# A transformer trunk in split float32r on one Trainium2 core: the weight tiles moved through all sixteen pairs of offsets modulo 128 bytes

## The chip, the cores and the metric

The kernel runs on one core of one Trainium2 chip. The metric is device time in microseconds (us) of one execution, from its first instruction to its last with what the device adds around them; smaller is better. Two timed executions of the kernel before took 2649.68 and 2650.5 us, median 2650.09 us.

## The reference

A decoder trunk of two layers, 256 tokens of width 2048, all float32. Layer 0 mixes tokens by retention (8 heads), layer 1 by sliding-window attention with sinks (32 query heads of 64, 4 key/value heads); each layer then has a SwiGLU feed-forward part (hidden width 5632) and a gated per-layer embedding (PLE, width 256):

```python
for i in range(DEPTH):
    h = rmsnorm(x, norm_mix[i])
    if i % N_MIXERS == 0:
        x = x + retention_mixer(h, ret_w_in[j], ret_gn[j], ret_w_out[j])
    else:
        x = x + swa_mixer(h, swa_w_in[j], swa_sinks[j], swa_w_out[j])
    x = x + swiglu(rmsnorm(x, norm_ffn[i]), ffn_w_in[i], ffn_w_out[i])
    gate = jax.nn.sigmoid(rmsnorm(x, norm_ple[i]) @ ple_w_gate[i])
    x = x + gate * (p[i] @ ple_w_proj[i])
return rmsnorm(x, norm_final)
```

Nearly all of the arithmetic is in the seven kinds of weight product: `ret_w_in` (2048 x 12288), `ret_w_out` (4096 x 2048), `swa_w_in` (2048 x 2560), `swa_w_out` (2048 x 2048), and per layer `ffn_w_in` (2048 x 11264), `ffn_w_out` (5632 x 2048), `ple_w_gate` (2048 x 2048) and `ple_w_proj` (256 x 2048).

## The kernel before

**Split operands.** A float32 matrix is split exactly into two float32r parts, hi and lo. A product of two matrices is then three TensorE products: hi by hi, hi by lo, lo by hi (L159 to L161 of `multiply`).

**Units.** A weight is cut into chunks of 512 output columns, and a chunk into units of 256 rows, 128 x 1024 float32 values in SBUF (512 KB). A unit takes one DMA on SP's queue into a `raw` tile (`load`, L125), one ScalarE activation that writes `hi` (L208) and one VectorE subtraction that writes `lo` (L209, both from `split_weights`, L133), and twelve matmuls: two blocks of 128 rows, two token tiles of 128, three products. In each of the twelve, 128 columns of the transposed activation are the stationary operand (loaded with an LDWEIGHTS of its own), and 512 columns of `hi` or `lo` are the moving one, one row of 2048 bytes in each partition. The stationary pairs are `xTh`/`xTl` (the normalised residual, for every product from the trunk), `yTh`/`yTl` (into `ret_w_out`), `hTh`/`hTl` (into `ffn_w_out`), `oTh`/`oTl` (into `swa_w_out`) and `pTh`/`pTl` (into `ple_w_proj`); each is an `Lhs` object, the trunk's with a new object per norm on the same two tiles.

**Order.** `run` (L163) goes through all units in one fixed order, one stage after another; loads are issued five units ahead (`LOADS`), splits three ahead (`AHEAD`), and after each unit one step of the side work is taken: transposes of finished chunks on VectorE (L233), norms, attention. Engines meet by semaphores on tiles that the tile pools hand out: five `raw`, four `hi`, four `lo`.

**Where tiles lie.** Every partition of SBUF is one address range; the pools take their tiles from it in the order in which they are opened, each tile rounded up to 32 bytes. `xs`, `ident`, `gains` and `gn` are multiples of 128 bytes long. `mhalf` (L103) has 16 bytes and takes 32, so that everything behind it, `xTh`, `xTl`, `pTh`, `pTl`, `raw`, `hi` and `lo`, starts 32 bytes past a multiple of 128. The pool `small` shifts what follows by 32 more: `xt`, `yT`, `hT`, `oT` and the retention's tiles start 64 bytes past a multiple of 128. Token tiles, row blocks and units are multiples of 512 bytes, so that an operand keeps its tile's offset in each matmul. In what follows, the offset of a tile is its address modulo 128 bytes, and the difference is the stationary operand's offset minus the moving one's, modulo 128.

The places that matter here are the pools and tiles at the head of `tile_trunk` (L90 to L106), `split_weights` (L133 to L139), `run`'s first lines (L166), the tiles of `yT`, `oT` and `hT` in the `opened` functions of `retention`, `swa` and `ffn`, and the tile `qkT` of a head's transposed queries and keys in `retention` (L318).

Of the kernel before, what the change touches and what calls it, by code (L numbers as in the profile page):

```python
# [11 lines left out]
F32 = mybir.dt.float32  # L12
# [6 lines left out]
P = 128  # L19
# [24 lines left out]
class Lhs:  # L44
    """A transposed activation, split exactly into two float32r parts."""

    def __init__(self, tiles=None):
        self.tiles = tiles
        self.ready = set()
# [5 lines left out]
class Chunk:  # L55
    """512 output columns for all tokens, accumulated over the whole contraction, in pieces of
    a token tile and some of the columns."""
# [7 lines left out]
class Unit:  # L65
    """KU blocks of 128 rows of a weight, in one chunk's columns."""

    def __init__(self, chunk, src, kts, lhs):
        self.chunk, self.src, self.kts, self.lhs = chunk, src, kts, lhs
        self.w = None  # L70


class Stage:
    """A part of the trunk with tiles of its own, from its first unit to its last."""
# [4 lines left out]
    def linear(self, w, block, lhs, done, units=None, chunk=None):  # L79
        """One chunk: block of 512 columns of a weight laid out by `_units`."""  # L80
        ch = chunk or Chunk(self, done)
        for u in units if units is not None else range(w.shape[1]):
            self.units.append(Unit(ch, w[block, u], range(KU * u, KU * u + KU), lhs))
            ch.left += 1
# [3 lines left out]
def tile_trunk(ctx, tc, ins, out):  # L88
    nc = tc.nc
    pool = ctx.enter_context(tc.tile_pool(name="persist", bufs=1))  # L90
    wraw = ctx.enter_context(tc.tile_pool(name="wraw", bufs=5))
    whi = ctx.enter_context(tc.tile_pool(name="whi", bufs=4))
    wlo = ctx.enter_context(tc.tile_pool(name="wlo", bufs=4))
    small = ctx.enter_context(tc.tile_pool(name="small", bufs=4))
# [3 lines left out]

    xs = pool.tile([P, NT, D], F32, name="xs")
# [3 lines left out]
    mhalf = pool.tile([P, 4], F32, name="mhalf")  # L103
    turned = ctx.enter_context(tc.tile_pool(name="turned", bufs=1))
    xT = [pool.tile([P, KD, S], F32R, name=n) for n in ("xTh", "xTl")]
    pT = [pool.tile([P, PLE_K, S], F32R, name=n) for n in ("pTh", "pTl")]  # L106

    # ---------------------------------------------------------------- streams
# [24 lines left out]
    def split_weights(u):  # L133
        raw = u.w
        hi = whi.tile([P, KU, NW], F32R, name="hi")
        lo = wlo.tile([P, KU, NW], F32R, name="lo")
        for part in u.parts:
            split(hi[:, part, :], lo[:, part, :], raw[:, part, :])
        u.w = (hi, lo)  # L139

    def multiply(u, which, left):
        """The unit's products for some pieces of its chunk; `left` of the chunk's units are
        still to come."""
        ch = u.chunk
        need(u.lhs, u.kts)
        if ch.acc is None:
            ch.acc = []
            for n, (_, cols) in enumerate(ch.pieces):
                bank, name = (ps_acc, "acc") if n < NT else (ps_at, "at")
                ch.acc.append(bank.tile([P, NW], F32, name=name)[:, : cols.stop - cols.start])  # L150
        hi, lo = u.w
        for j, k in enumerate(u.kts):
            first = not ch.begun and j == 0
            last = left == 0 and j == KU - 1
            for n in which:
                t, cols = ch.pieces[n]
                sl = slice(t * P, (t + 1) * P)
                xh, xl = u.lhs.hi[:, k, sl], u.lhs.lo[:, k, sl]
                nc.tensor.matmul(ch.acc[n], xh, hi[:, j, cols], start=first, stop=False)  # L159
                nc.tensor.matmul(ch.acc[n], xh, lo[:, j, cols], start=False, stop=False)  # L160
                nc.tensor.matmul(ch.acc[n], xl, hi[:, j, cols], start=False, stop=last)  # L161

    def run(stages, begin):  # L163
        """All units in order, their weights AHEAD units ahead; between them, steps of side work.
        The products of the units that end the last chunk go piece by piece of its output."""
        units = [(st, u) for st in stages for u in st.units]  # L166
        for n, (_, u) in enumerate(units[:LOADS]):
            if n < AHEAD:
                next(begin)
            load(u, 1 if n else KU)  # L170
            if n < AHEAD:
                split_weights(u)
        side.append(begin)
        now = None
        pools = ExitStack()
        last = [u for _, u in units[-AHEAD - 1 :]]
        assert len({id(u.chunk) for u in last}) == 1
        for i, (st, u) in enumerate(units):
            if st is not now:
                pools.close()  # L180
                st.open_(st, pools)
                now = st
            if i + LOADS < len(units):
                load(units[i + LOADS][1])
            if i + AHEAD < len(units):
                split_weights(units[i + AHEAD][1])
            if u is last[0]:
                break
            ch = u.chunk
            ch.left -= 1  # L190
            multiply(u, range(len(ch.pieces)), ch.left)
            ch.begun = True
            if ch.left == 0:
                g = ch.done(ch.acc)
                if g is not None:
                    side.append(g)
            step_side()
        ch = last[0].chunk
        for n, (t, cols) in enumerate(ch.pieces):
            for i, u in enumerate(last):  # L200
                multiply(u, [n], len(last) - 1 - i)
            ch.done(ch.acc[n], t, cols)
        pools.close()

    # ------------------------------------------------------------ small pieces
# [10 lines left out]
    def transpose_pair(srcs):  # L216
        """Two [128, 128] blocks of both token tiles -> a PSUM tile [128, 2, S]."""
        tr = ps_tr.tile([P, 2, S], F32, name="tr")
        for j, pair in enumerate(srcs):
            for t in range(NT):  # L220
                nc.tensor.transpose(tr[:, j, t * P : (t + 1) * P], pair[t], ident)
        return tr

    def transposes(dst, src):
        """Steps that transpose src [128, NT, 512] into dst [128, 4, S], by blocks of 32 x 32."""
# [11 lines left out]
    def blocks(src, i):  # L237
        """Blocks 2i and 2i + 1 of 128 columns of both token tiles."""
        return [[src(t)[:, b * P : (b + 1) * P] for t in range(NT)] for b in (2 * i, 2 * i + 1)]

    class Norm:
        """Sums of squares of the residual's chunks, and the transposed residual times the gain.
        The scale by token, inv, is applied behind the product with the weights."""
# [23 lines left out]
        def places(self, c, src):  # L267
            """Steps that put a chunk's four transposed blocks in place."""
            for j in range(4):
                if j % 2 == 0:  # L270
                    yield
                self.place(4 * c + j, src[:, j, :])
# [5 lines left out]
    def residual(stage, norm, c):  # L278
        """A chunk of an output projection onto the residual, then the next norm's part."""
# [16 lines left out]
    # --------------------------------------------------------------- retention  # L296
    def retention(norm, next_norm, w_in, w_out):
        yl = Lhs()

        def opened(st, pools):  # L300
            st.pool = pools.enter_context(tc.tile_pool(name="ret", bufs=2, reuse_waits="tile"))
            yl.tiles = [st.pool.tile([P, RET_OUT_K, S], F32R, name=n, bufs=1) for n in ("yTh", "yTl")]
# [3 lines left out]
        def head(h):  # L306
            st = {}

            def qk_done(acc):
# [7 lines left out]
                def later():  # L317
                    qkT = rp.tile([P, 4, S], F32, name="qkT", bufs=1)  # L318
# [77 lines left out]
    # ---------------------------------------------------- sliding-window attention  # L396
    def swa(norm, next_norm, w_in, w_out):
        ol = Lhs()
        st = {}

        def opened(stage, pools):
            sp = stage.pool = pools.enter_context(tc.tile_pool(name="swa", bufs=1, reuse_waits="tile"))
            ol.tiles = [sp.tile([P, KD, S], F32R, name=n) for n in ("oTh", "oTl")]
# [30 lines left out]
        def q_done_of(j):  # L434
            def q_done(acc):
# [12 lines left out]
                def scores(i):  # L448
                    """Of heads 2i and 2i + 1: the numerators and denominators' parts."""
# [100 lines left out]
        # The first chunks' last units wait for the last group of heads.  # L550
# [9 lines left out]
    # --------------------------------------------------------------------- FFN  # L560
    def ffn(layer, norm, next_norm):
        hl = Lhs()

        def opened(stage, pools):
            fp = stage.pool = pools.enter_context(tc.tile_pool(name="ffn", bufs=1, reuse_waits="tile"))
            hl.tiles = [fp.tile([P, FF_K, S], F32R, name=n) for n in ("hTh", "hTl")]
# [53 lines left out]
    # --------------------------------------------------------------------- PLE  # L620
    def ple(layer, norm, next_norm, final):
# [12 lines left out]
        def pair(c):  # L634
# [3 lines left out]
            def gate_done(acc):  # L638
# [7 lines left out]
                def later():  # L646
                    # The last reads of the old operand are queued: its place is free.
# [36 lines left out]
            def gate_last(acc, t, cols):  # L684
                """A piece of the last chunk; with a token tile's last one, its rows go out."""
# [39 lines left out]
    # ------------------------------------------------------------------- trunk  # L725
# [15 lines left out]
    def load_x():  # L741
        """The first norm's operand comes transposed, in step with the first chunk's weights."""
# [20 lines left out]
def _constants():  # L763
    """Tables that follow from the shapes alone."""
# [15 lines left out]
def _units(w):  # L780
    """[K, N] -> [N / 512, K / 256, 128, 2, 512]: each unit in one piece, by partitions."""
# [4 lines left out]
def _heads(w):  # L786
    """The retention's columns by heads: q and k, v, g."""
# [47 lines left out]
```

## Time and profile before

| what | value |
|---|---|
| median of the timed executions | 2650.09 us (2649.68 to 2650.5) |
| profiled execution, span from first to last instruction | 2647.9 us, 31279 instructions |
| TensorE busy (PE) | 2629.2 us, 99% of the span, 11632 matmuls |
| weight loads of TensorE (PEld) | 2142.7 us, 81% |
| VectorE (DVE) | 1817.2 us, 69% |
| ScalarE (ACT) | 1223.7 us, 46% |
| granted TensorE clock, mean of the core | 0.999 |
| DMA: share of the 16 engines' time of SP's queue | 58.5% |

The profiled execution's span is 2.2 us less than the median of the timed executions; those 2.2 us lie around the instructions. A matmul's duration in the profile is that of one instruction in a pipeline (0.39 us here) and overlaps its neighbours'; how fast matmuls follow each other is read from their starts, or from how many of them lie in a stretch in which TensorE is busy throughout. An LDWEIGHTS shows in the row PEld, and runs beside the matmul before the one that needs it.

### The profile page before, as it was taken

What the parts mean: (1) busy time and instruction counts of PE and PEld (TensorE: products, weight loads), DVE (VectorE), ACT (ScalarE), POOL (GpSimd) and SP (SyncE); (2) the same over time, 40 slices, a digit from 0 to 9 for tenths busy, and PEclk for the clock granted to TensorE, in tenths of its full rate; (3) what the DMA queues carried; (4) which work ended last, traced back from release to release, by engine and by line L of the source; (5) the groups of instructions that cost most, each with busy time, mean ns of one, the idle gap of its engine ahead of it and who ended that gap; (6) DMA issues with size and microseconds to landing.
All of it is one profiled execution on the core that took longest, in us unless ns stands there. A gap on an engine that the chain in (4) does not pass through costs nothing.

```text
span 2647.9 us, 31279 instructions
## 1 busy us (share of the span) xinstructions
PE 2629.2 (99%) x11632; PEld 2142.7 (81%) x11632; DVE 1817.2 (69%) x2567; ACT 1223.7 (46%) x1527; POOL 14.6 (1%) x30
## 2 busy tenths in 40 slices
PE   8999999999999999999999999999999999999998
PEld 6888888888888888888888887777888888888887
DVE  6777777766666667676555786888757575755565
ACT  6444444444444444444444555555444444444444
POOL 0000000000000000000000000000000000000000
PEclk9999999999999999999999999999999999999999
DMA  8555555565566565656655655346666666555564
GB/s 277 185 185 186 185 186 183 181 190 184 194 192 193 191 197 190 198 186 197 190 187 187 190 193 169 121 135 202 189 198 189 197 194 194 192 188 187 189 207 144
DMA packets 140506, 497.79 MB, mean 188 GB/s; under 512 B 15809, under 2 KB 19009, under 8 KB 140225
## 3 DMA queue, kind: packets, MB, share of 16 engines
q1 hardware_dynamic: 140064, 495.73, 58.5%
q8 instruction: 91, 1.49, 0.2%
q14 instruction: 63, 0.51, 0.1%
q10 hardware_dynamic: 288, 0.07, 0.0%
HBM read 493.63 MB, written 2.10 MB: 187 GB/s over the span
## 4 chain that ended last, share of the span: by engine, by line
PE 95%; DVE 3%; issue 1%; DMA 1%; ACT 0%; SPq 0%; ACTq 0%; POOLq 0%; POOL 0%; DVEq 0%
PE acc L159 31%; PE acc L161 31%; PE acc L160 31%; DVE lo L209 1%; DVE xt L233 1%; PE at L454 1%; PE tr L506 0%; PE at L532 0%; DMA raw<-in_ret_w_in 0%; PE at L323 0%; DVE xTl L212 0%; DVE qkT L233 0%; DMA xs<-in_x 0%; PE at L350 0%; PE at L352 0%
## 5 line engine op out<-in xcount | busy, mean ns | idle before, releaser
L209 DVE TENSOR_TENSOR lo<-raw,hi 128x1024 fp32r<-128x1024 f32 (+1 forms) x929 | 1131.8, 1221 | 720.2 <-ACT hi L208 712.8
L208 ACT ACTIVATE hi<-raw 128x1024 fp32r<-128x1024 f32 (+1 forms) x929 | 982.0, 1058 | 1210.9 <-PE acc L161 1117.4
L159 PE MATMUL acc<-hi,xTh 128*128 128x512 f32 x2592 | 1011.0, 390 | 6.6 <-ACT hi L208 5.4
L161 PE MATMUL acc<-hi,xTl 128*128 128x512 f32 x2592 | 1008.0, 389 | 0.8 <-DVE xTl L212 0.6
L160 PE MATMUL acc<-lo,xTh 128*128 128x512 f32 x2592 | 1008.7, 389 | 0.0
L159 PEld LDWEIGHTS acc<-hi,xTh 128*128 128x128 f32 x2592 | 487.3, 188 | 111.6 <-ACT hi L208 5.6
L161 PEld LDWEIGHTS acc<-hi,xTl 128*128 128x128 f32 x2592 | 487.0, 188 | 103.6 <-DVE xTl L212 2.5
L160 PEld LDWEIGHTS acc<-lo,xTh 128*128 128x128 f32 x2592 | 487.3, 188 | 100.5 <-issue 0.7
L161 PE MATMUL acc<-hi,hTl 128*128 128x512 f32 x704 | 278.4, 396 | 0.0
L160 PE MATMUL acc<-lo,hTh 128*128 128x512 f32 x704 | 278.4, 395 | 0.0
L159 PE MATMUL acc<-hi,hTh 128*128 128x512 f32 x704 | 278.4, 395 | 0.0
L233 DVE STREAM_TRANSPOSE xt<-h 32x256 f32<-32x256 f32 x352 | 153.6, 436 | 6.8
L161 PEld LDWEIGHTS acc<-hi,hTl 128*128 128x128 f32 x704 | 132.2, 188 | 32.1
L160 PEld LDWEIGHTS acc<-lo,hTh 128*128 128x128 f32 x704 | 132.2, 188 | 32.1
L159 PEld LDWEIGHTS acc<-hi,hTh 128*128 128x128 f32 x704 | 132.2, 188 | 31.9
L233 DVE STREAM_TRANSPOSE xt<-xs 32x256 f32<-32x256 f32 x320 | 139.5, 436 | 6.0
L161 PE MATMUL acc<-hi,yTl 128*128 128x512 f32 x256 | 101.2, 396 | 0.0
L160 PE MATMUL acc<-lo,yTh 128*128 128x512 f32 x256 | 101.2, 395 | 0.0
L159 PE MATMUL acc<-hi,yTh 128*128 128x512 f32 x256 | 101.2, 395 | 0.0
L233 DVE STREAM_TRANSPOSE qkT<-qk 32x256 f32<-32x256 f32 x128 | 55.8, 436 | 10.2 <-ACT qk L315 8.1
L211 ACT ACTIVATE xTh<-xt,gains 128x256 fp32r<-128x256 f32 x80 | 35.8, 499 | 56.0 <-DVE xt L233 51.6
L159 PEld LDWEIGHTS acc<-hi,yTh 128*128 128x128 f32 x256 | 48.1, 188 | 11.7
(124 smaller groups left out, 1178.2 us busy)
## 6 DMA issues: line engine op xcount, KB each, us to landing
raw<-in_ffn_w_in SPq DMA_DIRECT2D x352, 512.0 KB, 4.2
raw<-in_ret_w_in SPq DMA_DIRECT2D x191, 512.0 KB, 3.6
raw<-in_ffn_w_out SPq DMA_DIRECT2D x176, 512.0 KB, 4.0
raw<-in_ret_w_out SPq DMA_DIRECT2D x64, 512.0 KB, 4.0
raw<-in_ple_w_gate SPq DMA_DIRECT2D x64, 512.0 KB, 3.8
raw<-in_swa_w_in SPq DMA_DIRECT2D x40, 512.0 KB, 3.7
raw<-in_swa_w_out SPq DMA_DIRECT2D x32, 512.0 KB, 3.7
raw<-in_ple_w_proj SPq DMA_DIRECT2D x8, 512.0 KB, 4.0
```

The costliest lines, as they stand in the source:

```text
L159: nc.tensor.matmul(ch.acc[n], xh, hi[:, j, cols], start=first, stop=False)
L160: nc.tensor.matmul(ch.acc[n], xh, lo[:, j, cols], start=False, stop=False)
L161: nc.tensor.matmul(ch.acc[n], xl, hi[:, j, cols], start=False, stop=last)
L208: nc.scalar.activation(hi, src, AF.Copy)
L209: nc.vector.tensor_tensor(lo, src, hi.bitcast(F32), op=ALU.subtract)
L211: nc.scalar.activation(hi, src, AF.Copy, scale=scale)
L233: nc.vector.transpose(dst[b * SQ : (b + 1) * SQ, :, :, a, :], src[a * SQ : (a + 1) * SQ, :, :, b, :])
L454: nc.tensor.matmul(ats[e][:, 0:P] if b == 0 else ats[e][:, P : 3 * P], qT[sl, i, b * P : (b + 1) * P], kT[sl, j, 0 : (b + 1) * P], start=True,
```

## The change

The arithmetic, the instructions and their order on every engine stay as they are. What changes is where tiles lie.

1. `mhalf` takes 128 bytes, and the pools `whi` and `wlo` are opened ahead of `wraw`. `xTh`, `xTl` and `raw` then start at offset 0.
2. A helper `at_phase` makes a tile 128 bytes longer and returns the part that starts 32 bytes times a number `phase` behind the tile's start. `hi` and `lo` are made by it, their phases set per unit: among the units of one `Lhs` object, every four units (two for the attention's output product, `by_two`) step to the next of the sixteen pairs of phases (0 to 3) of `hi` and `lo`, `hi` stepping first.
3. The stationary pairs lie at one offset each: `xT` 0, `oT` 32, `yT` 64, `hT` and `pT` 96.
4. `qkT` no longer has a tile of its own in the retention's pool but takes the one tile `xt` of the pool `turned`, which the transposes of `y` and of the residual use too.
5. Comments and docstrings are taken out, so that line numbers move by up to 14.

Counted over the built programs by difference of stationary and moving offset (for each matmul on weights, the stationary tile that is loaded beside it against the rows that it streams):

| difference, bytes mod 128 | 0 | 32 | 64 | 96 |
|---|---|---|---|---|
| before: matmuls | 7919 | 3264 | 0 | 0 |
| with the change: matmuls | 2829 | 2475 | 2769 | 3110 |

Before, the 7919 are those on `xT` and `pT`, the 3264 those on `hT`, `yT` and `oT`. With the change, about one unit in fifteen (250 of 3728 pairs of a `hi` and a `lo` matmul) has both `hi` and `lo` at the offset of its stationary tile.

On VectorE the order of a retention head's transposes is the same; only the tile's name differs. Before, around the end of the first head (`yTl` is the split of the transposed `y`, L233 a transpose, L209 a weight split):

```order
L233 STREAM_TRANSPOSE xt<-y 32x2x4x32 x2
L209 TENSOR_TENSOR lo<-raw,hi 128x1024
L212 SCALAR_TENSOR_TENSOR yTl<-xt,gn,yTh 128x256 x4
L209 TENSOR_TENSOR lo<-raw,hi 128x1024 x3
L233 STREAM_TRANSPOSE qkT<-qk 32x2x4x32 x3
```

The transposes of the next head's queries and keys stand three weight splits behind the last reader of `xt` on this engine. The same place with the change:

```order
L246 STREAM_TRANSPOSE xt<-y 32x2x4x32 x2
L222 TENSOR_TENSOR lo<-raw,hi 128x1024
L225 SCALAR_TENSOR_TENSOR yTl<-xt,gn,yTh 128x256 x4
L222 TENSOR_TENSOR lo<-raw,hi 128x1024 x3
L246 STREAM_TRANSPOSE xt<-qk 32x2x4x32 x3
```

No row moved; the last one now writes the tile that the third one reads.

The diff, without the comments and docstrings:

```diff
 class Lhs:
     def __init__(self, tiles=None):
         self.tiles = tiles
+        self.by_two = False
         self.ready = set()
...
 class Unit:
     def __init__(self, chunk, src, kts, lhs):
         self.chunk, self.src, self.kts, self.lhs = chunk, src, kts, lhs
         self.w = None
+        self.phase = (0, 0)
...
 def tile_trunk(ctx, tc, ins, out):
     nc = tc.nc
     pool = ctx.enter_context(tc.tile_pool(name="persist", bufs=1))
-    wraw = ctx.enter_context(tc.tile_pool(name="wraw", bufs=5))
     whi = ctx.enter_context(tc.tile_pool(name="whi", bufs=4))
     wlo = ctx.enter_context(tc.tile_pool(name="wlo", bufs=4))
+    wraw = ctx.enter_context(tc.tile_pool(name="wraw", bufs=5))
...
+    def at_phase(pool, shape, dtype, name, phase, **kw):
+
+        n = shape[1] * shape[2]
+        t = pool.tile([P, n + 32], dtype, name=name, **kw)[:, 8 * phase : 8 * phase + n]
+        return t.rearrange("p (a b) -> p a b", b=shape[2])
+
...
-    mhalf = pool.tile([P, 4], F32, name="mhalf")
+    mhalf = pool.tile([P, 32], F32, name="mhalf")[:, 0:4]
     turned = ctx.enter_context(tc.tile_pool(name="turned", bufs=1))
     xT = [pool.tile([P, KD, S], F32R, name=n) for n in ("xTh", "xTl")]
-    pT = [pool.tile([P, PLE_K, S], F32R, name=n) for n in ("pTh", "pTl")]
+    pT = [at_phase(pool, [P, PLE_K, S], F32R, n, 3) for n in ("pTh", "pTl")]
...
     def split_weights(u):
         raw = u.w
-        hi = whi.tile([P, KU, NW], F32R, name="hi")
-        lo = wlo.tile([P, KU, NW], F32R, name="lo")
+        hi = at_phase(whi, [P, KU, NW], F32R, "hi", u.phase[0])
+        lo = at_phase(wlo, [P, KU, NW], F32R, "lo", u.phase[1])
...
     def run(stages, begin):
         units = [(st, u) for st in stages for u in st.units]
+        count = {}
+        for _, u in units:
+            n = count[id(u.lhs)] = count.get(id(u.lhs), -1) + 1
+            g = n // (2 if u.lhs.by_two else 4)
+            u.phase = g % 4, g // 4 % 4
...
-            yl.tiles = [st.pool.tile([P, RET_OUT_K, S], F32R, name=n, bufs=1) for n in ("yTh", "yTl")]
+            yl.tiles = [at_phase(st.pool, [P, RET_OUT_K, S], F32R, n, 1, bufs=1) for n in ("yTh", "yTl")]
...
-                    qkT = rp.tile([P, 4, S], F32, name="qkT", bufs=1)
+                    qkT = turned.tile([P, 4, S], F32, name="xt")
...
         ol = Lhs()
+        ol.by_two = True
...
-            ol.tiles = [sp.tile([P, KD, S], F32R, name=n) for n in ("oTh", "oTl")]
+            ol.tiles = [at_phase(sp, [P, KD, S], F32R, n, 0) for n in ("oTh", "oTl")]
...
-            hl.tiles = [fp.tile([P, FF_K, S], F32R, name=n) for n in ("hTh", "hTl")]
+            hl.tiles = [at_phase(fp, [P, FF_K, S], F32R, n, 2) for n in ("hTh", "hTl")]
```

## The prediction

> **What bounds the kernel now.** I read the busy times first, then the waits, then the pace of the matmuls stage by stage, then single matmuls in order of time. Busy times and the chain of work that ended last:
>
> ```profile
> PE 2629.2 (99%) x11632; PEld 2142.7 (81%) x11632; DVE 1817.2 (69%) x2567; ACT 1223.7 (46%) x1527; POOL 14.6 (1%) x30
> PE 95%; DVE 3%; issue 1%; DMA 1%; ACT 0%; SPq 0%; ACTq 0%; POOLq 0%; POOL 0%; DVEq 0%
> ```
>
> TensorE is busy for 99% of the span and carries 95% of the chain. The groups by line give its matmuls by stationary tile, with what TensorE idled before them in the last column (of the three products of each tile I show the first; the other two have the same counts):
>
> ```profile
> L159 PE MATMUL acc<-hi,xTh 128*128 128x512 f32 x2592 | 1011.0, 390 | 6.6 <-ACT hi L208 5.4 <-ACT xTh L211 1.2
> L159 PE MATMUL acc<-hi,hTh 128*128 128x512 f32 x704 | 278.4, 395 | 0.0
> L159 PE MATMUL acc<-hi,yTh 128*128 128x512 f32 x256 | 101.2, 395 | 0.0
> L159 PE MATMUL acc<-hi,oTh 128*128 128x512 f32 x128 | 51.6, 405 | 0.0
> L159 PE MATMUL acc<-hi,pTh 128*128 128x512 f32 x32 | 12.4, 389 | 0.0
> ```
>
> Three times these counts: 7776 + 96 = 7872 matmuls with a stationary tile at offset 32 (`xT`, `pT`), and 3 x (704 + 256 + 128) = 3264 with one at offset 64 (`hT`, `yT`, `oT`). They wait for almost nothing, so the time is the number of matmuls times their pace. The pace comes from stretches in which TensorE is busy throughout, the first on `xT`, the second on `hT`:
>
> ```profile
> core 0: us, PE busy (x) PEld busy (x) DVE busy (x) ACT busy (x) POOL busy (x), PEclk, DMA share, GB/s
> 800.00:1200.00 400.00, 400.00 (x1767) 331.31 (x1766) 264.81 (x329) 178.14 (x186) 0.00 (x0) 1.00 0.61 194
> 1240.00:1440.00 200.00, 200.00 (x859) 161.01 (x858) 115.83 (x137) 84.27 (x96) 0.00 (x0) 1.00 0.59 188
> ```
>
> Two of each count began before the stretch. So `xT` has 400 us / 1765 = 226.6 ns from one matmul to the next, and `hT` has 200 us / 857 = 233.4 ns, at the same granted clock (1.00), with the same moving tiles and shape. Six or seven ns per matmul thus hang on something about the stationary tile. Its offset is one candidate: `xT` stands at the moving tiles' own offset (difference 0), `hT` 32 bytes past it (difference 32).
>
> The third view is what tells me that difference 0 is a lock-in and not simply a faster pair. In order of time, right after four transposes in the attention stage, on `xT` throughout (start in us, duration, instruction):
>
> ```profile
> 1593.76 0.40 PE L160 MATMUL acc<-lo,xTh 128*128 128x512 f32 x1
> 1593.99 0.40 PE L161 MATMUL acc<-hi,xTl 128*128 128x512 f32 x1
> 1594.22 0.40 PE L159 MATMUL acc<-hi,xTh 128*128 128x512 f32 x1
> 1594.46 0.39 PE L160 MATMUL acc<-lo,xTh 128*128 128x512 f32 x1
> 1594.68 0.39 PE L161 MATMUL acc<-hi,xTl 128*128 128x512 f32 x1
> 1594.91 0.40 PE L159 MATMUL acc<-hi,xTh 128*128 128x512 f32 x1
> 1595.15 0.39 PE L160 MATMUL acc<-lo,xTh 128*128 128x512 f32 x1
> 1595.38 0.40 PE L161 MATMUL acc<-hi,xTl 128*128 128x512 f32 x1
> 1595.61 0.39 PE L159 MATMUL acc<-hi,xTh 128*128 128x512 f32 x1
> 1595.84 0.39 PE L160 MATMUL acc<-lo,xTh 128*128 128x512 f32 x1
> ```
>
> The steps between starts vary between 0.22 and 0.24 us although offsets, lengths and clock are those of the steady stretch; nine of them take 1595.84 - 1593.76 = 2.08 us, 231.1 ns each. After that the pace is the steady one again. So a matmul's length depends on how its reads fall against something, presumably the weight load that runs beside it, and at difference 0 a run of equal matmuls settles into the cheapest repeating pattern that the trace shows.
>
> **The change part by part.** No instruction is added, removed or moved. Four effects are to be priced.
>
> *Matmuls on differences that are known.* By the table of the change, difference 0 falls from 7919 to 2829 matmuls, difference 32 from 3264 to 2475; 5879 go to differences 64 and 96, which no weight matmul before has.
>
> *Matmuls on unknown differences, and the mixing.* In 15 of 16 pairs of offsets `hi` and `lo` don't both stand at the stationary tile's offset, and within twelve matmuls the moving tile then often jumps between two offsets. What a locked run pays is therefore not what I take; I take the unlocked pace, 231.1 ns, for every matmul outside the one unit in fifteen (0.067) that has all three tiles at one offset, and 226.6 ns for those. The bounds for the unseen differences are the extreme steps of the rows above: 0.22 us below, 0.24 us above. A second place supports a value in the middle. The retention's small products have both operands at offset 64 (difference 0, but neither at 32), three in a row:
>
> ```profile
> 60.25 0.39 PE L350 MATMUL at<-vh,prh 128*128 128x512 f32 x1
> 60.48 0.39 PE L351 MATMUL at<-vl,prh 128*128 128x512 f32 x1
> 60.71 0.39 PE L352 MATMUL at<-vh,prl 128*128 128x512 f32 x1
> 60.94 0.39 PE L159 MATMUL acc<-hi,xTh 128*128 128x512 f32 x1
> ```
>
> They take (60.94 - 60.25) / 3 = 230 ns each: not cheaper for standing at a multiple of 64, and like the unlocked pace. So I reckon by difference and pattern, and not by the absolute offset.
>
> The sum: before, 7872 x 226.6 + 3264 x 233.4 = 1783.8 + 761.8 = 2545.6 us. With the change, 0.067 x 11136 = 746 matmuls at 226.6 and 10390 at 231.1: 169.0 + 2401.1 = 2570.1 us. The difference is +24.5 us: the 7872 lose up to 4.5 ns each (about 33 us), the 3264 win 2.3 (about 8 us).
>
> *VectorE and ScalarE* read `raw` and write `hi` and `lo` at changed offsets. I price this at nothing. Two groups differ in just this, the split of `xT` from `raw` (same offset as `xTh`) and from `xt` (32 bytes off); the third row is the weight split:
>
> ```profile
> L212 DVE SCALAR_TENSOR_TENSOR xTl<-xt,gains,xTh 128x256 fp32r<-128x256 f32 x80 | 34.3, 479 | 5.2 <-ACT xTh L211 5.2
> L212 DVE SCALAR_TENSOR_TENSOR xTl<-raw,gains,xTh 128x256 fp32r<-128x256 f32 x16 | 7.0, 479 | 3.5 <-ACT xTh L211 3.5
> L209 DVE TENSOR_TENSOR lo<-raw,hi 128x1024 fp32r<-128x1024 f32 x927 | 1130.5, 1222 | 718.7 <-ACT hi L208 711.4
> ```
>
> It is 479 ns both times. The cover is wide: a unit of twelve matmuls takes 12 x 226.6 = 2719 ns, of which VectorE is busy 264.81 / 400, or 1800 ns. The split, 1222 ns, could grow by 900 ns before TensorE waited; were it to double, each unit would pay some 300 ns, 929 units 280 us.
>
> *`qkT` in the shared tile.* The new wait is that the transposes of a head's queries and keys must find `xt` free. Its readers, the splits into `yTh` (ScalarE) and `yTl` (VectorE), are ahead of them in VectorE's own queue, with three weight splits between, 3 x 1222 ns. Nothing waits longer. If it did, the queue behind would be weight splits issued three units ahead, 3 x 2.7 us of cover, in eight places; at most a few us.
>
> The profiled execution is 2647.9 us with 2.2 us around it to the median of the runs. 2647.9 + 2.2 + 24.5 = **2675 us**, 0.9% above 2650.1. A measurement of this kernel tells about 2% (53 us) from no change, so the forecast counts as within 2%.
>
> **The rivals.** (1) *The unseen differences are cheap.* If 64 and 96 keep the weight load's reads out of the way, their 5879 matmuls go at the shortest step, 220 ns, and the known ones stay at their locked pace: 2829 x 226.6 + 2475 x 233.4 + 5879 x 220 = 2512.1 us against 7919 x 226.6 + 3264 x 233.4 = 2556.3, that is -44 us, **2606 us**, not slower than before. For it: steps of 0.22 us occur. Against: only singly, each followed by long ones. It is decided by whether such steps can follow each other. To be faster by over 2% they would have to go below 218.5 ns, which no row shows.
>
> (2) *The mixing is dear.* Every jump between two offsets starts the pattern anew at its costly end. Place: the step from `lo` back to `hi`, twice in three matmuls. With the pace halfway from 231.1 to the longest step, 240 ns, namely 235.6, for 0.933 of 11183 matmuls, the total is 2458.2 + 169.7 = 2627.9, +72 us, **2722 us**. It counts as slower from 233.8 ns on, just above what `hT` pays steadily at 233.4. Against it: nine steps of an unlocked run average 231.1.
>
> (3) *It is not the offset.* `hT`, `yT` and `oT` also lie at higher addresses than `xT`, and are read in other stages. Then each stage keeps its pace, and the time stays at **2650 us**. For it: offset and place go together in every long stretch. Against: the varying steps on one and the same tile. The Trainium skill speaks for it: the page "TensorE: Matmul & The Clock Gate", section "Part 2: What happens when you issue a matmul", has two independent SBUF read ports in TensorE, so that loading the next weights takes nothing from the running matmul; offsets of the two would then not matter at all. By that rule the sum of the change is nil; the two paces of 226.6 and 233.4 ns on the same moving tiles already sit badly with it.
>
> **How the numbers follow.** Forecast 0.55, rival 1 0.18, rival 2 0.15, rival 3 0.12. Of rival 1 I give 0.05 to more than 2%; rival 2 counts as slower with 0.12 of its 0.15, and 0.02 of the forecast's spread lies there too. Faster 0.05, within 2% 0.81, slower 0.14. The range takes in the forecast, rival 3, the greater part of rival 1 (one of two unseen differences cheap: half of -44 us, 2628) and most of the way to rival 2: 2620 to 2720.
>
> **What would show it.** Right: stretches on `xT` of about 231 ns per matmul on average, with paces that change every four units between about 226 and 236; `hT` a little below 233.4; TensorE still 99% busy; L209 still at 1222 ns; the order and the waits of the retention as before. Wrong: stretches of four units at 220 ns or less (rival 1), long stretches above 234 (rival 2), `xT` at 226.6 and `hT` at 233.4 throughout (rival 3), or TensorE waiting for `lo`.

## The result and the profile after

The changed kernel took 2682.39 us (median of two, 2682.22 to 2682.55) against 2650.09 us, a ratio of 1.0121 with a 95% interval of 1.0091 to 1.0150. That is 32.3 us more, where 2675 us, 24.5 us more, had been forecast.

The busy times of the profiled execution after (span 2680.4 us), from its page:

```profile
PE 2662.0 (99%) x11632; PEld 2145.2 (80%) x11632; DVE 1818.0 (68%) x2567; ACT 1223.9 (46%) x1527; POOL 14.6 (1%) x30
```

The count of matmuls is the same, and TensorE's busy time is 32.8 us longer, which is the whole loss. VectorE and ScalarE have not moved. The pace, from the same two stretches as before, the first on `xT`, the second on `hT` (us of the stretch, PE's busy time with the matmuls it held, clock):

```profile
core 0: us, PE busy (x), PEclk, DMA share, GB/s
800.00:1200.00 400.00, 400.00 (x1727) 1.00 0.62 189
1240.00:1440.00 200.00, 200.00 (x865) 1.00 0.63 189
```

Less the two that began earlier, 400 / 1725 = 231.9 ns on `xT` (before 226.6) and 200 / 863 = 231.7 ns on `hT` (before 233.4). On average both stretches have come to nearly one pace, close to the 231.1 ns that the prediction took for a run without its lock. Single units don't go at one pace: the experiments below show how it depends on the offsets. The weight split, whose operands now stand at four offsets, is unchanged (line by form, VectorE):

```profile
L222 DVE TENSOR_TENSOR lo<-raw,hi 128x1024 fp32r<-128x1024 f32 x927 | 1130.8, 1222 | 747.3 <-ACT hi L221 739.9
```

So the direction and nearly the size were right. What was open is why. The table in front counts 2829 matmuls at difference 0 modulo 128, but the longer tiles also put the four buffers of `hi` and `lo` 4224 bytes apart, so that modulo 256 their addresses alternate between two values 128 apart. If the period that counts were 256 bytes, the lengthening alone would already cost something, without any stepping.

### The profile page after: what moved, and what is told of

Its sections match the earlier page's. It is cut to its first block, busy times and chain, and to the rows that moved or that the text cites. A ratio compares the mean times of both kernels' runs of the same rounds, so it can differ in the third digit from the quotient of the medians.

```text
span 2680.4 us, 31287 instructions
## 1 busy us (share of the span) xinstructions
PE 2662.0 (99%) x11632; PEld 2145.2 (80%) x11632; DVE 1818.0 (68%) x2567; ACT 1223.9 (46%) x1527; POOL 14.6 (1%) x30
## 4 chain that ended last, share of the span: by engine, by line
PE 95%; DVE 2%; issue 1%; DMA 1%; ACT 0%; SPq 0%; ACTq 0%; POOLq 0%; POOL 0%; DVEq 0%
PE acc L167 31%; PE acc L169 31%; PE acc L168 31%; DVE xt L246 1%; DVE lo L222 1%; PE at L468 1%; PE tr L520 0%; PE at L546 0%; DMA raw<-in_ret_w_in 0%; PE at L336 0%; DMA xs<-in_x 0%; PE at L365 0%; PE at L364 0%; PE at L363 0%; ACT hi L221 0%
## 5 line engine op out<-in xcount | busy, mean ns | idle before, releaser
L167 PE MATMUL acc<-hi,xTh 128*128 128x512 f32 x2592 | 1023.8, 395 | 6.5 <-ACT hi L221 5.8
L169 PE MATMUL acc<-hi,xTl 128*128 128x512 f32 x2592 | 1020.3, 394 | 0.4 <-DVE xTl L225 0.4
L168 PE MATMUL acc<-lo,xTh 128*128 128x512 f32 x2592 | 1020.5, 394 | 0.0
L246 DVE STREAM_TRANSPOSE xt<-qk 32x256 f32<-32x256 f32 x128 | 55.8, 436 | 11.2 <-ACT qk L328 9.1
L246 DVE STREAM_TRANSPOSE xt<-y 32x256 f32<-32x256 f32 x128 | 55.8, 436 | 2.5
```

The costliest lines, as they stand in the source:

```text
L246: nc.vector.transpose(dst[b * SQ : (b + 1) * SQ, :, :, a, :], src[a * SQ : (a + 1) * SQ, :, :, b, :])
```

## The experiments

Three questions: is it the difference of the two offsets at all (and not the place or the stage), what is its period, and does each matmul pay for its own pair or does a run as a whole lose a pattern? Times are medians beside runs of the kernel before on the same chip.

| run | edit | us | before | ratio, 95% interval |
|---|---|---|---|---|
| e1_all_zero | difference 0 everywhere, at offset 160 mod 256 | 2629.88 | 2650.68 | 0.9922 (0.9907 to 0.9937) |
| e2_no_steps | changed kernel, no stepping | 2672.59 | 2650.68 | 1.0083 (1.0066 to 1.0100) |
| e3_map_both | `hi` and `lo` step together by 16 bytes | 2683.76 | 2650.68 | one run |
| e4_map_lo | only `lo` steps by 16 bytes | 2681.08 | 2650.68 | one run |
| e5_qkt | kernel before, `qkT` in `xt` alone | 2649.72 | 2650.34 | 0.9999 (0.9990 to 1.0008) |
| e6_fine | `hi` and `lo` step together by 4 bytes | 2692.97 | 2650.34 | one run |
| e7_step_256 | changed kernel, buffers a multiple of 256 apart | 2680.68 | 2650.34 | 1.0117 (1.0101 to 1.0134) |
| e8_all_at_0 | difference 0 everywhere, at offset 0 mod 256 | 2630.22 | 2650.06 | 0.9926 (0.9909 to 0.9943) |
| e9_minus16 | weights 16 bytes before, everywhere | 2712.04 | 2650.06 | one run |

### Is it the difference? The stationary tiles moved by 32 bytes

The smallest edit to the kernel before: the 32 bytes of the warm-up tile in `small` go, and all pools behind it move up.

```diff
-    mhalf = pool.tile([P, 4], F32, name="mhalf")
+    mhalf = pool.tile([P, 8], F32, name="mhalf")
...
-    nc.vector.memset(mhalf, -0.5)
-    warm = small.tile([P, 4], F32, name="warm", bufs=1)
-    nc.scalar.activation(warm, mhalf, AF.Copy)
+    nc.vector.memset(mhalf[:, 0:4], -0.5)
+    nc.scalar.activation(mhalf[:, 4:8], mhalf[:, 0:4], AF.Copy)
```

> The kernel before, with yT, oT, hT and the retention's tiles moved by 32 bytes so that every stationary tile lies at the weight tiles' own offset (difference 0; the warm-up tile is gone, so the pools behind it move). Theory A (the pace hangs on the difference of stationary and moving offset, and difference 0 locks at 226.6 ns): the 3264 matmuls on yT, oT and hT fall from 233.4 to 226.6 ns, 22 us less than before, about 2628 us. Rival B (the pace hangs on the place of the tile or on the stage): they stay at 233.4 ns, 2650 us.

Measured: 2629.88 us, 20.8 us less than the kernel before. The two stretches of this kernel:

```profile
core 0: us, PE busy (x) PEld busy (x) DVE busy (x) ACT busy (x) POOL busy (x), PEclk, DMA share, GB/s
800.00:1200.00 400.00, 400.00 (x1767) 331.20 (x1766) 263.79 (x327) 178.18 (x186) 0.00 (x0) 1.00 0.59 194
1240.00:1440.00 200.00, 200.00 (x884) 165.60 (x883) 118.18 (x140) 86.33 (x98) 0.00 (x0) 1.00 0.62 193
```

The second, on `hT`, now holds 884 matmuls instead of 859: 200 / 882 = 226.8 ns, the pace of `xT`. Of the operands of the weight products only the stationary tiles have moved, by 32 bytes. 6.6 ns off each of 3264 matmuls make 21.5 us, about the whole gain of 20.8. A higher place in memory and the stage are ruled out as causes, since both are as before.

Does the place of the pair count when the difference is 0? The same kernel with `mhalf` at 128 bytes has all tiles at offset 0 modulo 256:

```diff
-    mhalf = pool.tile([P, 8], F32, name="mhalf")
+    mhalf = pool.tile([P, 32], F32, name="mhalf")
```

> As the first experiment, difference 0 everywhere, but with all tiles at offset 0 modulo 256 instead of 160. Theory (only the difference counts): the same, 2630 us. Rival (a row of 2048 bytes that starts at a multiple of 128 is read in one block less): below 226.6 ns per matmul, 2600 us or less.

Measured 2630.22 us, the same within the interval. A row that starts on a multiple of 256 bytes is no cheaper than one that doesn't. Its two stretches hold the same counts as the first experiment's:

```profile
800.00:1200.00 400.00, 400.00 (x1767) 1.00 0.59 194
1240.00:1440.00 200.00, 200.00 (x884) 1.00 0.61 194
```

### Which period? The changed kernel without its steps

```diff
-            u.phase = g % 4, g // 4 % 4
+            u.phase = 0, 0
```

> The changed kernel with every unit at phase (0, 0): longer tiles and new places, but no stepping. The weight buffers are then 4224 bytes apart, so that their addresses modulo 256 alternate between 0 and 128. Theory A128 (only the difference modulo 128 counts): xT stays at difference 0 and at 226.6 ns, the rest near 232, about 2645 us. Theory A256 (the difference modulo 256 counts, and 128 is as dear as others, 233 ns): units on xT alternate between 227 and 233 ns with the buffer, mean 230, so 7776 x 3.5 ns = 27 us more than before less some 5 us on the others, about 2672 us. Rival (the stepping makes the whole loss): 2650 us.

Measured 2672.59 us, against 2672 by the theory of 256 bytes and 2645 by that of 128. About two thirds of the loss (21.9 of 32.3 us) is there although no tile steps. One can see it unit by unit. The first, second and fourth of these rows are the first matmuls of three units on `xT`, in order of time; the third is the second unit's fourth matmul:

```profile
900.72 0.40 PE L167 MATMUL acc<-hi,xTh 128*128 128x512 f32 x1
...
903.51 0.39 PE L167 MATMUL acc<-hi,xTh 128*128 128x512 f32 x1
...
904.21 0.39 PE L167 MATMUL acc<-hi,xTh 128*128 128x512 f32 x1
...
906.25 0.40 PE L167 MATMUL acc<-hi,xTh 128*128 128x512 f32 x1
```

The first unit lies in a buffer 128 bytes off `xT` modulo 256 and takes 2.79 us for its twelve matmuls, 232.5 ns each; the next lies at difference 0 and takes 2.74 us, 228 ns: its first three steps 0.70 us, 233 ns each, the other nine 2.04 us, 226.7 ns each. They alternate like this throughout the stretch.

The counterpart keeps the stepping and takes away the buffers' odd distance:

```diff
-        t = pool.tile([P, n + 32], dtype, name=name, **kw)[:, 8 * phase : 8 * phase + n]
+        t = pool.tile([P, n + (64 if pool in (whi, wlo) else 32)], dtype, name=name, **kw)[:, 8 * phase : 8 * phase + n]
```

> The changed kernel with weight buffers 4352 bytes apart instead of 4224, so that their distance is a multiple of 256 and only the stepping varies the difference on xT. If the two losses add, the stepping's own loss is what the whole change lost less what the buffers' distance lost alone, 32 - 22 = 10 us, 2660 us. If a run that has once lost its lock has nothing more to lose, stepping alone costs nearly all, 2678 to 2683 us.

Measured 2680.68 us, 30.3 us over the kernel before. The new places without stepping cost 21.9 us, the stepping with buffers a multiple of 256 apart costs 30.3, both together 32.3: they don't add. Either one takes most of the runs on `xT` out of their lock, and there is little more to lose. What remains isn't one pace, though. These rows are the first matmuls of four groups of four units in this kernel:

```profile
930.02 0.39 PE L167 MATMUL acc<-hi,xTh 128*128 128x512 f32 x1
...
940.93 0.40 PE L167 MATMUL acc<-hi,xTh 128*128 128x512 f32 x1
...
952.13 0.39 PE L167 MATMUL acc<-hi,xTh 128*128 128x512 f32 x1
...
963.22 0.39 PE L167 MATMUL acc<-hi,xTh 128*128 128x512 f32 x1
```

The first group has `hi` and `lo` at `xT`'s offset; its 48 matmuls take 10.91 us, 227.3 ns each. In the next two `lo` stays there and `hi` stands 32, then 64 bytes off: 11.20 us, 233.3 ns, and 11.09 us, 231.0 ns. The loss is an average over such paces.

### The map: sixteen offsets, hi and lo together

From the first experiment, with `hi` and `lo` tiles of 4096 + 256 bytes (buffers a multiple of 256 apart), `qkT` in `xt` to make room, and each stationary tile's units in sixteen groups:

```diff
+        of = {}
+        for _, u in units:
+            of.setdefault(id(u.lhs), []).append(u)
+        for same in of.values():
+            for n, u in enumerate(same):
+                g = n * 16 // len(same)
+                u.phase = (g, g)
...
+        t = pool.tile([P, n + 64], dtype, name=name)[:, 4 * phase : 4 * phase + n]
```

> A map: all stationary tiles at one offset modulo 256, weight buffers 4352 bytes apart (a multiple of 256), hi and lo of a unit at the same offset, which steps through the sixteen multiples of 16 bytes, each for a sixteenth of the units of a stationary pair in one go (11 or 12 units on xT). Theory A256: the first sixteenth is at 226.6 ns, steps of 32 bytes at 231 to 233, 128 bytes at 233; mean 232, total about 2688 us. Theory A128: the ninth sixteenth (128 bytes) is at 226.6 ns too. Rival: the pace does not follow the step.

Measured 2683.76 us. Five of the sixteen groups in the first feed-forward stage, on `xT`, 22 us in the middle of each (at 0, 16, 64, 160 and 240 bytes):

```profile
core 0: us, PE busy (x), PEclk, DMA share, GB/s
758.00:780.00 22.00, 22.00 (x98) 1.00 0.60 191
788.00:810.00 22.00, 22.00 (x97) 1.00 0.54 171
...
880.00:902.00 22.00, 22.00 (x98) 1.00 0.57 181
...
1064.00:1086.00 22.00, 22.00 (x95) 1.00 0.55 188
...
1218.00:1240.00 22.00, 22.00 (x99) 1.00 0.61 197
```

The counts of 95 to 99 are the whole spread; finer are the mean steps from start to start in the same trace, over all of a group's matmuls (moving minus stationary offset in bytes modulo 256; the front's difference is this with its sign turned):

| bytes | 0 | 16 | 32 | 48 | 64 | 80 | 96 | 112 | 128 | 144 | 160 | 176 | 192 | 208 | 224 | 240 |
|---|---|---|---|---|---|---|---|---|---|---|---|---|---|---|---|---|
| `xT`, ns | 227.5 | 231.6 | 233.4 | 233.2 | 229.0 | 231.1 | 233.5 | 231.0 | 232.4 | 233.2 | 234.2 | 232.5 | 233.2 | 234.1 | 233.2 | 229.3 |
| `yT`, ns | 226.7 | 231.6 | 233.4 | 233.2 | 229.2 | 231.0 | 233.6 | 231.0 | 232.4 | 233.3 | 234.3 | 233.3 | 233.1 | 234.5 | 233.3 | 226.8 |
| `hT`, ns | 227.2 | 231.6 | 233.4 | 233.2 | 229.1 | 231.0 | 233.5 | 231.0 | 232.5 | 233.3 | 234.1 | 231.1 | 233.3 | 234.7 | 233.3 | 226.8 |

Three tiles in three stages give the same figure within 0.3 ns at twelve of the sixteen offsets. That is the strongest sign that the two offsets set the pace. 224 bytes is `hT`'s relation in the kernel before: 233.3 here, 233.4 there. At 128 bytes there is no second minimum, as the theory of 256 bytes has it; the 229 ns at 64 bytes it had not foreseen. A period longer than 256 bytes isn't needed either: these buffers lie 4352 bytes apart, 17 times 256, so that their addresses alternate modulo 512, and `yT` at difference 0 still goes at 226.7 ns. The mean over all, 232.0 ns, is close to what the changed kernel pays (231.9 and 231.7).

### Does each matmul pay for itself? Only lo stepped

The same kernel with `u.phase = (0, g)`.

> As the map, but hi stays at difference 0 and only lo steps through the sixteen multiples of 16 bytes. If each matmul pays for its own pair of offsets, one matmul in three pays what the map shows, so the mean is a third of the way from 226.6 to the map's pace, near 228.5 ns, and the total about 2650 us. If a jump between two offsets costs by itself, the pace is 231 or more wherever lo is off, and the total about 2675 us or more.

Measured 2681.08 us. The stretch on `xT` of this kernel:

```profile
800.00:1200.00 400.00, 400.00 (x1724) 1.00 0.59 189
```

400 / 1722 = 232.3 ns, as much as when `hi` steps too. Two of three matmuls have difference 0 here, and they go at 231.4 ns all the same (mean of some 5000 uninterrupted steps on `xT` that start with a matmul on `hi`, among them the one sixteenth in which `lo` matches too). Even the steps from one matmul on `hi` to the next on `hi` take 231.1 ns. The price is not one matmul's own: a single moving tile off the pattern in three takes the lock from the other two.

### Finer, and a theory that fell: steps of 4 bytes

The map from -32 to +28 bytes (slices `phase : phase + n`, and spare tiles that move the weights by 224 bytes and the stage pools to match).

> The map in steps of 4 bytes: moving minus stationary offset from -32 to +28 bytes modulo 256, hi and lo of a unit alike, a sixteenth of the units each. Theory L (two offsets count as matching when they fall into the same line of 16 bytes or the line behind it): 226.7 ns flat from -16 to 0 and about 231 to 233 ns outside. Rival S (a smooth dependence): a single best step between -16 and 0, below 226.7 ns. Total 2670 to 2680 us by either.

Measured 2692.97 us, and both theories fell. The mean steps on `xT`:

| bytes | -32 | -28 | -24 | -20 | -16 | -12 | -8 | -4 | 0 | 4 | 8 | 12 | 16 | 20 | 24 | 28 |
|---|---|---|---|---|---|---|---|---|---|---|---|---|---|---|---|---|
| ns | 233.3 | 236.7 | 234.6 | 228.4 | 233.4 | 239.5 | 231.8 | 228.0 | 226.9 | 237.7 | 233.4 | 228.9 | 231.6 | 238.6 | 233.5 | 227.4 |

It is neither flat within 16 bytes nor smooth: 4 bytes off on one side cost 11 ns, on the other 1 ns. None is cheaper than 0. And the figure at -16 contradicts the first map (226.8 on `yT` and `hT` there). Two stretches of this one kernel on `xT`, both at -16 bytes:

```profile
158.00:180.00 22.00, 22.00 (x99) 1.00 0.59 191
...
882.00:904.00 22.00, 22.00 (x95) 1.00 0.53 174
```

99 matmuls against 95 in the same time: 22 / 97 = 226.8 ns and 22 / 93 = 236.6 ns, at the same addresses modulo 256, the same stationary tile and the same clock. One pair of offsets has more than one steady pace. In both maps the groups follow each other in the same order, so that a figure away from 0 may belong to the pair together with what ran before it.

### Several patterns for one pair of offsets

The map's kernel with `u.phase = (15, 15)` for all units, -16 bytes throughout.

> hi and lo of all units start 16 bytes before the stationary tile's offset modulo 256, throughout. Theory M (this pair of offsets has several repeating patterns, and the phase at which a run of matmuls starts decides which it falls into): stretches at 226.7, 233.3 and 236.7 ns, constant within a run and changing only where other matmuls or a wait come between; total between 2630 us (all cheap) and 2740 us (all at 236.7). Rival N (the paces of the two maps differed by something else, as the history of the buffers): one pace throughout.

Measured 2712.04 us, and the paces are constant within long runs. Two stretches:

```profile
600.00:1000.00 400.00, 400.00 (x1716) 1.00 0.58 189
1900.00:2300.00 400.00, 400.00 (x1692) 1.00 0.57 185
```

400 / 1714 = 233.4 ns and 400 / 1690 = 236.7 ns. In the trace one run of 4548 matmuls without interruption goes at 233.3 ns from end to end, through stages on `xT`, `yT` and `hT`, and one of 3613 at 236.7 ns; in the retention, where small products interrupt, the pace changes between 236.7 and 233.3 at these interruptions and nowhere else. That is the expectation of theory M. Its third pace shows in a short run at the start: 17 steps from 19.21 to 23.07 us, 227 ns each. At difference 0 no long run was seen to settle at anything but 226.7, in any of these kernels.

### The shared tile alone

```diff
-                    qkT = rp.tile([P, 4, S], F32, name="qkT", bufs=1)
+                    qkT = turned.tile([P, 4, S], F32, name="xt")
```

> The kernel before with the change's fourth point alone: the transposed queries and keys of a retention head take the shared tile xt. Theory: the wait for the tile is over before the transposes come up in VectorE's queue, so nothing, 2650 us. Rival: each of the eight heads waits for the split of the head before, a few us in all, 2653 us or more.

Measured 2649.72 us against 2650.34: nothing, as expected. What these transposes wait for in its trace is the same, 8.0 us for ScalarE's `qk` against 8.1 in the kernel before.

## Why the prediction was right, and where it was off

**TensorE's pace is the whole effect.** Right: busy time +32.8 us for a loss of 32.3, with the other engines unchanged.

**Difference 0 is a lock-in; unlocked runs go at 231 ns.** The lock at difference 0 is right: with a single tile in three off it, the whole run slows. That there is one unlocked pace is not. The nine steps behind the 231.1 ns, and the 230 ns of the retention's small products, are matmuls at difference 0 on their way back to the lock after an interruption. What the changed kernel pays, 231.9 and 231.7 ns in the two stretches, is an average over units whose twelve matmuls go at means from 227 to 235.5 ns, by the offsets of `hi` and `lo` together. Nothing in the prediction ties the one figure to the other, so that it was partly luck that they lie within 1 ns. Over all uninterrupted steps the matmuls on `xT` and `pT` went from 226.9 to 231.8 ns: 7872 x 4.9 = 38.6 us, where about 33 had been forecast.

**One unit in fifteen keeps 226.6 ns.** Off. The count went by 128 bytes, and the period of difference 0 is larger: at 128 the map has 232.4 ns. With buffers an odd multiple of 128 apart, half of the units that the table counted as matching on `xT` don't match, and `yTh`/`yTl` and `hTh`/`hTl`, now themselves 128 apart, can't both match. Of 928 units 62 match by 128 bytes, 24 by 256. The units that do match spend their first matmuls on finding the lock (2.74 us instead of 12 x 226.6 = 2.72 in the second experiment).

**The high-offset tiles win.** Right: `hT` went from 233.4 to 231.7 ns in its stretch, 1.7 instead of the 2.3 forecast. Over all uninterrupted steps `hT`, `yT` and `oT` went from 233.3 to 231.8 ns: 3264 x 1.5 = 4.9 us, where about 8 had been forecast. The two terms then give 38.6 - 4.9 = 33.7 us, near the 32.3 measured. So both terms were mis-sized, and both towards a faster kernel than was measured. The 7776 matmuls on `xT` also hold 48 of only 256 columns, too few to matter.

**Edits priced at nothing.** VectorE's split took 1222 ns before and after; the shared tile cost nothing by itself.

**The signs.** Paces that change along `xT` were seen, but from unit to unit instead of every four units, because the buffers alternate.

**Rivals.** (1) Cheap unseen differences: none below 226.7 ns in steps of 16 bytes, nor around 0 in steps of 4; of the other multiples of 32 the best is a moving tile 64 bytes ahead, at 229. (2) Dear mixing: mixing does take the lock away (only `lo` off: 232.3 ns), but leads to the same 232, not beyond 233.8. (3) Not the offset: refuted, since 32 bytes on the stationary tiles alone were worth 20.8 us. The Trainium skill's sentence behind it ("TensorE: Matmul & The Clock Gate", "Part 2: What happens when you issue a matmul": loading the next weights takes no read bandwidth from the running matmul) would leave the place of the stationary rows without effect. Here only that place was moved, and the pace went from 233.4 to 226.8 ns, so that a pace worked out by it would be wrong for these matmuls; whether it is the read bandwidth that they share, no run shows.

**Shown and not shown.** Shown: equal offsets modulo 256 give 226.7 ns, 128 bytes apart don't; away from that the pace hangs on the offsets of all tiles in a run together and not on one matmul's pair, and how a run starts can decide between several paces. Only argued: that what meets is the read of the weight load with the read of the moving rows. No run separated the two reads in time, and what in the chip has the period of 256 bytes, or why 4 bytes matter, stays open.

## What to carry to other kernels

In a stream of float32r matmuls like these (128 x 128 by 128 x 512, a weight load each), give stationary and moving tiles the same address modulo 256 bytes, buffers included (distance between buffers a multiple of 256): here 32 bytes less in a small pool were worth 0.8%, and the kernel so changed beats both. Padding a tile for any other reason can undo this silently: 128 bytes more per weight buffer and the new places that came with them cost 21.9 us. To price a change of addresses, don't average single pairs; look for the pace of runs, and how long after an interruption they take to settle.

## What the runs showed of the hardware that was not expected

- At the same offsets, clock and shape, runs of matmuls hold one of several paces: 233.3 ns over 4548 matmuls and 236.7 ns over 3613 in one kernel, changing only where a run was interrupted, and 226.8 or 236.6 ns in two stretches of another.
- Offsets of 4 bytes matter: +4 bytes 237.7 ns, -4 bytes 228.0 ns, 0 bytes 226.9 ns.
- In twelve matmuls at difference 0 after a unit at 128 bytes, the lock is back after about three (233 ns a step, then 226.7).
